# Two transformer blocks on one core: bias loads a unit ahead, u and v in one pass, work spread differently between units

## The chip, the cores and the metric

The kernel runs on one core of one Trainium2 chip. The metric is the device time of one execution in microseconds (us). The core has a matrix engine (TensorE, PE), a vector engine (VectorE, DVE), a scalar engine (ScalarE, ACT), GpSimd (POOL) and SyncE (SP), which here only issues DMAs. Each engine works through its own list of instructions in order; ACT issues some DMAs too.

## The reference, cut to what matters

x is 512 tokens by 1024. The first block adds a mixer, an attention to 256 memory rows and a feed-forward part; the second block has two layers and a second stream, a context of 256 rows, which is computed beside x.

```python
h = rms_norm(x, norm_mix_g)
u, v, q, kv, gl = split(h @ w_in)
a = spatial_gating_unit(gelu(u), gelu(v), ...)
b = nsa_attention(q, kv, gl, ...)
x = x + concat(rms_norm(a), rms_norm(b)) @ w_out
x = x + memory_cross_attention(rms_norm(x), mem, ...)
x = x + square(relu(rms_norm(x) @ w_ff1)) @ w_ff2
for l in range(2):
    m, mc = silu(c) @ w_mod[l] + b_mod[l], silu(c_ctx) @ w_mod[l] + b_mod[l]
    x, xc = ffn(x, m, 0), ffn(xc, mc, 0)
    # mixers on h @ w_in[l]: gated convolution, pooling, and
    # neighbourhood attention: softmax(q k * scale + bias, and context keys)
    x = x + m[5] * mixers(mod_norm(x, m, 1), context keys and values of xc)
    x, xc = ffn(x, m, 2), ffn(xc, mc, 2)      # xc in layer 0 alone
out = rms_norm(x, final_g)
```

mod_norm is an RMS norm with a scale and a shift from the nine rows of m (the conditioning).

## The kernel before, in words

All large products run in three parts: an input h is held as a rounded half and a remainder, each weight tile likewise (whi, wlo), and PE adds whi·h, whi·remainder and wlo·h (L375 to L377 and its kin). A weight tile of 512 KB comes by DMA on SP into one of three buffers (`prefetch`, L330); `ensure` (L334) then lets ACT make whi (L345) and DVE wlo (L346), and `get` (L349) hands out the next tile and sees to the split of the ones behind it. The order of all engines' instructions is the order in which the program calls them; there is no scheduler behind it. So the program works in units (a head and a block of rows, for example), and between two units it puts other work by hand:

- `queue` holds generators; `fill(ns)` (L242) advances the first one until its own estimates of cost sum to ns. A negative cost stops it. The context stream (`ctx_chain`, L1332) is such a generator, and so is the memory's key and value projection (`mem_kv`).
- `after(n, f)` and `sides` are run by `step` (L266), once per unit: postponed pieces and side generators.
- `tick` (L554) does one part of the conditioning: a DMA of 256 KB on ACT's queue into one of two buffers (`wm`) and a product with a sum on DVE (L579). `need_mods` (L595) does as many parts as are lacking where the rows are needed.

In block 1, `project_qk` (L793) makes q and the keys; its `stat` sums squares per head on PE (L848) one step after the product, and `finish_k` (L806) scales the keys and stacks their halves (L817 to L820) in one go. After that v is projected, u is projected as filler between the units of `nsa` (L1003) by `project_u` (L874) with its gelu at the end (L888), and `spatial` (the gating) follows u. Then come the memory attention (`mem_attention`, L1201), and the feed-forward part.

In block 2, `norm_now` (L504) makes a norm of x: sums over columns on PE (L465), a root on POOL and DVE, a spread of the row factors over partitions on PE (L474), then a product on DVE (L496), a sum and cast on ACT (L497) and the remainder on DVE (L499), tile by tile. Between these it fills, and it also calls `ensure`. It is written (l, i) below: norm i of layer l. `attend` (L1670) is the neighbourhood attention of 8 heads by 4 blocks: for each unit `a` computes scores on PE (L1695) and adds the bias on DVE (L1696), `e` is the exponential on ACT (L1703), `bb` transposes on PE (L1710) and copies on ACT (L1712), `cc` multiplies with v (L1724). `pipeline` (L619) lets `bb` and `cc` trail `a` by a given number of units (2 and 2). The bias is loaded in the unit that adds it:

```python
m, pr, bt = self.small(1), tmp(), bias[j % 2]
nc.sync.dma_start(bt[:, :256], self.d["bias"][l, (0, 1, 1, 2)[j], hd])
```

`stack` (L1651) prepares the next head in three steps, one per unit. The first makes halves of q on ACT (L1659) and DVE (L1660) and at once issues two DMAs on SP that copy them crosswise (L1662, L1663). `attend_spread` (L1811) does layer 1's attention with the rest of the mixers as filler.

Of the kernel before, what the change touches and what calls it, by code (L numbers as in the profile page):

```python
# [8 lines left out]
F32 = mybir.dt.float32  # L9
F32R = mybir.dt.float32r  # L10
# [6 lines left out]
T = 512  # L17
TC = 256
# [7 lines left out]
FILL_NSA, FILL_MEM, FILL_MIX, FILL_NA = 1900, 3650, 1350, 900  # L26
FILL_A, FILL_S, FILL_B, FILL_FFN, FILL_END, FILL_U = 1300, 4000, 2500, 0, 700, 4000
# [185 lines left out]

class Body:
    def __init__(self, ctx, tc, d, out, pk, at, order):
        self.ctx, self.tc, self.nc, self.d, self.out, self.pk, self.at = ctx, tc, tc.nc, d, out, pk, at
        enter = ctx.enter_context
        self.const = enter(tc.tile_pool(name="const", bufs=1))
        self.base = enter(tc.tile_pool(name="base", bufs=1))
        self.wp = enter(tc.tile_pool(name="wp", bufs=3))  # L220
        self.tp = enter(tc.tile_pool(name="tp", bufs=5))
        self.sp = enter(tc.tile_pool(name="sp", bufs=10))
        self.pp = enter(tc.tile_pool(name="pp", bufs=5, space=bass.MemoryType.PSUM))
        self.hs = [[self.base.tile([128, 8, n], F32R, tag=f"h{n}{i}", name="h") for i in range(2)] for n in (T, TC)]
        self.order = order
        self.used = []
# [59 lines left out]

    def t2(self, n=512):
        return self.tp.tile([128, 528], F32, tag="t2", name="t2")[:, :n]
# [44 lines left out]

    def ensure(self, i):  # L334
        order = self.order
        while len(self.split) <= min(i, len(order) - 1):
# [4 lines left out]
            hi = self.wp.tile([128, 1024], F32R, tag="whi", name="whi")[:, :nk * nc]  # L341
            lo = self.wp.tile([128, 1024], F32R, tag="wlo", name="wlo")[:, :nk * nc]
# [6 lines left out]
    def get(self, key, tick=1, ahead=2):  # L349
        i = len(self.used)  # L350
        self.used.append(key)
        if self.order is None:
            _, _, nk, nc = self.pk.pieces[key]
            w = [self.wp.tile([128, 1024], F32R, tag=t, name=t)[:, :nk * nc] for t in ("whi", "wlo")]
# [280 lines left out]
    def block1(self):  # L635
# [7 lines left out]
        nc.scalar.copy(warm, warm)  # L643
        for k in range(8):
# [10 lines left out]
        mem = base.tile([128, 8, TC], F32, tag="xc", name="mem")  # L655
# [3 lines left out]
        with tc.tile_pool(name="b1", bufs=1) as self.b1:  # L659
            with tc.tile_pool(name="mix1", bufs=1) as mp:  # L660
# [54 lines left out]
                self.queue += [comp, memkv]  # L715
                for cc in range(2):
                    ps = [self.mm() for _ in range(4)]
                    for half in range(2):
                        self.gemm_tm([(ps[b][:, :256], hh[:, :, b * 128:(b + 1) * 128], hl[:, :, b * 128:(b + 1) * 128])
                                      for b in range(4)], self.get(("v", cc, half)), 4 * half, 8)  # L720
                        self.fill(2000)
                        next(memkv)
                    for b in range(4):
                        nc.scalar.activation(vv[:, b, cc * 256:(cc + 1) * 256], ps[b][:, :256], AF.Gelu_apprx_tanh,
                                             scale=pair[:, 0, b:b + 1])
                self.finish(comp)
                gu = self.project_u(hh, hl, u, vv, rows, pair)
                mh, ml = self.new_h()
                yc = self.keep(2)
                self.chain = self.ctx_chain(yc)  # L730
                sg = self.spatial(u, vv, sgw, mh, ml)
                self.queue.insert(0, gu)
                self.queue.append(self.chain)
                pre = self.ctx_rstd(yc)
                self.sides.append(pre)
                for n, c in enumerate(self.nsa(qs, kh, kl, v2, gates, kc, vc, st_q, mh, ml)):
                    self.fill(FILL_U if n < 10 else FILL_NSA)
                    if self.parts < 48:
                        self.tick()
                    if n == 10:  # L740
                        self.finish(gu)
                        self.sides.append(sg)
                    if n == 14:
                        self.run(pre)
# [48 lines left out]
    def project_qk(self, hh, hl, qs, st_q, kh, kl, gg, x, ss, pair):  # L793
# [12 lines left out]
        def finish_k():  # L806
            for i in range(2):
# [8 lines left out]
                for h in range(2):  # L816
                    nc.scalar.copy(kh[half[h], h, i], k[half[h]])  # L817
                    nc.vector.tensor_copy(kh[half[1 - h], h, i], k[half[h]])
                    minus(kl[half[h], h, i], k[half[h]], kh[half[h], h, i])
                    nc.scalar.copy(kl[half[1 - h], h, i], kl[half[h], h, i].bitcast(F32))  # L820

        for n, m in enumerate((4, 5, 6, 7, 2, 3)):
# [32 lines left out]
            self.after(1, stat)  # L855
# [18 lines left out]
    def project_u(self, hh, hl, u, vv, rows, pair):  # L874
        nc = self.nc
        ln = self.layer_norm(vv, rows)
        for cc in range(2):
            ws = [self.get(("u", cc, half), 1, 2 - half) for half in range(2)]
            for b in range(4):
                next(ln, None)  # L880
                p = self.mm()[:, :256]
                bs = slice(b * 128, (b + 1) * 128)
                for half in range(2):
                    self.gemm_tm([(p, hh[:, :, bs], hl[:, :, bs])], ws[half], 4 * half, 8)
                nc.scalar.activation(u[:, b, cc * 256:(cc + 1) * 256], p, AF.Copy, scale=pair[:, 0, b:b + 1])
                yield 2600
        for b in range(4):
            nc.scalar.activation(u[:, b], u[:, b], AF.Gelu_apprx_tanh)  # L888
# [465 lines left out]
    def ffn2(self, l, f, with_x, with_c, norm_c=None, halves=None):  # L1354
# [103 lines left out]
    def norm_c(self, l, i, slow=True, y=None):  # L1458
# [4 lines left out]
        for _ in self.norm(self.xc, TC, None if y is not None else self.ssc, g, sh, *self.hc, slow=slow, y=y):  # L1463
            yield 1500
# [186 lines left out]
    def stack(self, hd, q_t, k_t):  # L1651
# [9 lines left out]
        halves(q1, q_t[hs, t])  # L1661
        nc.sync.dma_start(q2[os].bitcast(F32), q1[hs].bitcast(F32))  # L1662
# [7 lines left out]
    def attend(self, q_t, k_t, v_t, vc, l, first, mixed, bias, tmp, tmp_t, rows, ready=lambda: True):  # L1670
# [9 lines left out]

        def a(un):
# [10 lines left out]
            nc.sync.dma_start(bt[:, :256], self.d["bias"][l, (0, 1, 1, 2)[j], hd])  # L1692
# [56 lines left out]
        yield from self.pipeline(units, a, bb, cc, 2, 2, e=e)  # L1749
# [173 lines left out]
```

## Time and profile before

| what | value |
|---|---|
| median of 3 runs | 3551.75 us (3551.11 to 3552.49) |
| profiled execution, its time | 3544.91 us |
| its span | 3543.2 us |
| mean granted TensorE clock, as a share of 2.4 GHz | 0.976 |
| PE busy | 3393.7 us, 96% |
| DVE, ACT, POOL busy | 58%, 34%, 3% |

The span goes from the first to the last instruction of one profiled execution; its time is 1.7 us longer than its span. A busy engine is one with an instruction in it, so PE at the lower of its two clocks (1.2 GHz, a granted clock of 0.50) is as busy as at the upper.

### The profile page before, as it was taken

Reading aid. Unit: us, or ns where it says so; the run is one execution under the profiler, and the core shown is the slowest. Engines: PE = TensorE matmul, PEld = TensorE weight load, DVE = VectorE, ACT = ScalarE, POOL = GpSimd, SP = SyncE. Lnnn points to the kernel's source line nnn. Section 1 sums busy time; section 2 is a strip of 40 time slices with the busy share of each in tenths; the row PEclk is TensorE's granted clock in tenths of the full one; section 3 lists DMA queues with packets and bytes.
Section 4 is the critical chain, followed back from the end, with each engine's and each line's share of the span. In section 5 each row is a group of like instructions: output and inputs, shape, how many; then the busy total and the mean of one; then the engine's idle time right before and its main releaser. Section 6 shows DMA issues by size and latency. Waiting matters only on the chain.

```text
span 3543.2 us, 48186 instructions
## 1 busy us (share of the span) xinstructions
PE 3393.7 (96%) x18878; PEld 2960.0 (84%) x18878; DVE 2039.8 (58%) x4231; ACT 1219.0 (34%) x2423; POOL 105.9 (3%) x156
## 2 busy tenths in 40 slices
PE   8979999999999999979999999999999998899999
PEld 6878888888888888878888888888888887778887
DVE  5587666656776677655655555554444454454445
ACT  5445445433332224354421222231222134432222
POOL 1000000000000001000000000100000010000000
PEclk9989999999999999999999999999999999899999
DMA  5533343444444443433333333223323223223332
GB/s 174 185 124 127 112 130 125 141 145 146 146 143 143 144 147 116 155 91 99 102 91 98 98 90 98 75 90 99 96 92 96 68 72 115 61 68 104 101 96 78
DMA packets 143348, 396.79 MB, mean 112 GB/s; under 512 B 16144, under 2 KB 27280, under 8 KB 142608
## 3 DMA queue, kind: packets, MB, share of 16 engines
q1 hardware_dynamic: 94736, 305.61, 27.3%
q10 hardware_dynamic: 48384, 88.10, 8.5%
q8 instruction: 148, 2.42, 0.3%
q14 instruction: 80, 0.66, 0.1%
HBM read 387.36 MB, written 2.10 MB: 110 GB/s over the span
## 4 chain that ended last, share of the span: by engine, by line
PE 84%; DVE 7%; ACT 4%; issue 3%; DMA 2%; POOL 0%; SPq 0%; ACTq 0%; DVEq 0%; POOLq 0%
PE mm L375 19%; PE mm L376 19%; PE mm L377 19%; PE aux L375 5%; PE aux L376 5%; PE aux L377 5%; DVE wlo L346 2%; PE aux L1724 1%; PE mm L404 1%; PE mm L403 1%; PE mm L405 1%; PE mm L388 1%; PE mm L1710 1%; PE mm L389 1%; DMA bias<-in_bias 1%
## 5 line engine op out<-in xcount | busy, mean ns | idle before, releaser
L346 DVE TENSOR_TENSOR wlo<-raw,whi 128x512 fp32r<-128x512 f32 (+1 forms) x1060 | 694.4, 698 | 447.6 <-ACT whi L345 439.3
L345 ACT CAST whi<-raw 128x512 fp32r<-128x512 f32 (+1 forms) x1060 | 599.7, 616 | 938.6 <-issue 773.5
L375 PE MATMUL mm<-h,whi 128*128 128x512 f32 (+1 forms) x2352 | 901.2, 383 | 14.6 <-ACT whi L345 14.6
L376 PE MATMUL mm<-h,whi 128*128 128x512 f32 (+1 forms) x2352 | 895.9, 381 | 0.0
L377 PE MATMUL mm<-h,wlo 128*128 128x512 f32 (+1 forms) x2352 | 894.3, 380 | 0.3 <-DVE wlo L346 0.2
L375 PEld LDWEIGHTS mm<-h,whi 128*128 128x128 f32 x2352 | 449.4, 191 | 97.5 <-ACT whi L345 15.0
L377 PEld LDWEIGHTS mm<-h,wlo 128*128 128x128 f32 x2352 | 448.2, 191 | 84.8 <-DVE wlo L346 1.3
L376 PEld LDWEIGHTS mm<-h,whi 128*128 128x128 f32 x2352 | 449.0, 191 | 79.1 <-issue 0.9
L375 PE MATMUL aux<-h,whi 128*128 128x256 f32 x1056 | 304.0, 288 | 0.0
L376 PE MATMUL aux<-h,whi 128*128 128x256 f32 x1056 | 300.3, 284 | 0.5 <-DVE h L499 0.3
L377 PE MATMUL aux<-h,wlo 128*128 128x256 f32 x1056 | 299.9, 284 | 0.0
L375 PE MATMUL mm<-g,whi 128*128 128x512 f32 (+1 forms) x720 | 277.9, 386 | 0.0
L376 PE MATMUL mm<-g,whi 128*128 128x512 f32 (+1 forms) x720 | 277.7, 386 | 0.0
L377 PE MATMUL mm<-g,wlo 128*128 128x512 f32 (+1 forms) x720 | 276.7, 384 | 0.0
L579 DVE CUSTOM_DVE_ANT_0 wm<-wm,silu_c 128x512 f32<-128x512 f32 x336 | 232.2, 692 | 19.8 <-DMA wm<-in_wmod 13.6
L1384 DVE SCALAR_TENSOR_TENSOR x<-mm,gate,x 128x512 f32<-128x512 f32 x160 | 119.9, 749 | 159.1 <-PE mm L377 159.0
L376 PEld LDWEIGHTS aux<-h,whi 128*128 128x128 f32 x1056 | 203.6, 193 | 5.0 <-DVE h L499 1.3
L375 PEld LDWEIGHTS aux<-h,whi 128*128 128x128 f32 x1056 | 203.7, 193 | 4.1 <-issue 0.3
L377 PEld LDWEIGHTS aux<-h,wlo 128*128 128x128 f32 x1056 | 203.4, 193 | 0.0
L408 ACT CAST g<-t 128x512 fp32r<-128x512 f32 x88 | 54.6, 621 | 396.6 <-DVE t L1430 396.6
L1430 DVE SCALAR_TENSOR_TENSOR t<-t,mm 128x512 f32<-128x512 f32 x88 | 60.6, 688 | 183.7 <-PE mm L377 183.1
L377 PEld LDWEIGHTS mm<-g,wlo 128*128 128x128 f32 x720 | 135.3, 188 | 27.5
(368 smaller groups left out, 4951.1 us busy)
## 6 DMA issues: line engine op xcount, KB each, us to landing
raw<-in_w_a SPq DMA_DIRECT2D x220, 512.0 KB, 3.5
wm<-in_wmod ACTq DMA_DIRECT2D x336, 256.0 KB, 2.7
raw<-in_w_d SPq DMA_DIRECT2D x110, 512.0 KB, 3.5
raw<-in_w_in SPq DMA_DIRECT2D x84, 512.0 KB, 3.6
raw<-in_w_f SPq DMA_DIRECT2D x64, 512.0 KB, 3.5
raw<-in_w_out SPq DMA_DIRECT2D x32, 512.0 KB, 3.5
bias<-in_bias SPq DMA_DIRECT2D x64, 128.0 KB, 2.2
fc<-in_cw SPq DMA_DIRECT2D x8, 512.0 KB, 4.8
```

The costliest lines, as they stand in the source:

```text
L345: self.nc.scalar.copy(hi[:, cs], raw[:, cs])
L346: self.nc.vector.tensor_tensor(lo[:, cs], raw[:, cs], hi[:, cs].bitcast(F32), op=OP.subtract)
L375: mmul(o, wh[:, k, cols], h[:, k], start=s, stop=False)
L376: mmul(o, wh[:, k, cols], l[:, k], start=False, stop=False)
L377: mmul(o, wl[:, k, cols], h[:, k], start=False, stop=e)
L388: mmul(o, wh[:, k], h[:, k], start=n == 0, stop=False)
L389: mmul(o, wl[:, k], h[:, k], start=False, stop=False)
L403: mmul(o, h[:, k0 + k], wh[:, k], start=s, stop=False)
L408: self.nc.scalar.copy(hi, src)
L579: nc.vector.tensor_tensor_reduce(o, w, self.sc[:, s, ks], 1.0, 0.0, OP.mult, OP.add, wm[:, half, s, j % 8:j % 8 + 1])
L1384: nc.vector.scalar_tensor_tensor(xs, o, gate[:, m:m + 1], xs, op0=OP.mult, op1=OP.add)
L1430: nc.vector.scalar_tensor_tensor(hid, hid, 0.5, b, op0=OP.mult, op1=OP.mult)
```

## The change

It has these parts; lines are those of the kernel before, or of the kernel after where it says so.

1. `project_uv` computes v, then u, with the gelu straight out of PSUM, before the attention units, beside the compression, `mem_kv`, the context's sums and the layer norm; `spatial` becomes a side generator from the start of NSA, and the queue holds `mem_kv` and the context chain alone. NSA's fill goes from 1900 (4000 in its first ten units) to 2700 a unit; the context's norm reports 2700 a step in place of 1500.
2. `stat` runs two steps after its product; the stacking of the keys becomes six steps of a side generator.
3. At the start DVE sets the memory tile's first part to 1 and PE multiplies it with itself five times; nobody reads the result, and the memory's load waits for it.
4. `busy(3)`: three products of constants that nobody reads, at up to three places of `norm_now`, if the queue is empty. `ensure` leaves `norm_now` for the feed-forward part's last down products, whose weights (`kept`) are put into two buffers of a pool of their own.
5. In `attend` the bias of unit n+1 is loaded in unit n, and the first one ahead of the loop; the crosswise copies of q are issued one step later, after the halves of k; the lag of `bb` goes from 2 to 3, that of `cc` behind it from 2 to its default 1.

```diff
-FILL_NSA, FILL_MEM, FILL_MIX, FILL_NA = 1900, 3650, 1350, 900
+FILL_NSA, FILL_MEM, FILL_MIX, FILL_NA = 2700, 3650, 1350, 900
...
+    def busy(self, n):
+        p = self.mm()
+        for _ in range(n):
+            self.nc.tensor.matmul(p[:, :256], self.ident, self.cst[:, :256], start=True, stop=True)
...
+    def split_tiles(self, kept, n):
+        pool, bufs = (self.fp, 2) if kept else (self.wp, None)
+        return [pool.tile([128, 1024], F32R, tag="k" * kept + t, name=t, bufs=bufs)[:, :n] for t in ("whi", "wlo")]
...
     def norm_now(self, ready, *args):
+        if not self.queue:
+            self.busy(3)
         self.fill(FILL_A)
         it = self.norm(*args)
         next(it)
+        if not self.queue:
+            self.busy(3)
         self.fill(FILL_S)
         while not ready():
             self.fill(1000)
-        if self.order:
-            self.ensure(len(self.used) + 1)
-        for _ in it:
+        for n, _ in enumerate(it):
+            if n == 0 and not self.queue:
+                self.busy(3)
             self.fill(FILL_B / 4)
...
+        mem = base.tile([128, 8, TC], F32, tag="xc", name="mem")
+        idle = mem.rearrange("p k n -> p (k n)")[:, :512]
+        nc.vector.memset(idle, 1.0)
+        p = self.mm()
+        for _ in range(5):
+            nc.tensor.matmul(p, idle[:, :128], idle, start=True, stop=True)
...
+                pre = self.ctx_rstd(yc)
+                ln = self.layer_norm(vv, rows)
+                for n, _ in enumerate(self.project_uv(hh, hl, u, vv, pair)):
+                    self.step()
+                    next(comp, None)
+                    if n < 4:
+                        next(memkv)
+                    else:
+                        next(pre, None)
+                    if n % 4 == 3:
+                        next(memkv)
+                        next(memkv)
+                    if n > 7:
+                        next(ln, None)
+                for g in (comp, ln, pre):
+                    self.run(g)
                 sg = self.spatial(u, vv, sgw, mh, ml)
-                self.queue.insert(0, gu)
-                self.queue.append(self.chain)
-                pre = self.ctx_rstd(yc)
-                self.sides.append(pre)
-                for n, c in enumerate(self.nsa(qs, kh, kl, v2, gates, kc, vc, st_q, mh, ml)):
-                    self.fill(FILL_U if n < 10 else FILL_NSA)
+                self.sides.append(sg)
+                self.queue += [memkv, self.chain]
+                for c in self.nsa(qs, kh, kl, v2, gates, kc, vc, st_q, mh, ml):
+                    self.fill(FILL_NSA)
...
-                for h in range(2):
-                    nc.scalar.copy(kh[half[h], h, i], k[half[h]])
-                    nc.vector.tensor_copy(kh[half[1 - h], h, i], k[half[h]])
-                    minus(kl[half[h], h, i], k[half[h]], kh[half[h], h, i])
-                    nc.scalar.copy(kl[half[1 - h], h, i], kl[half[h], h, i].bitcast(F32))
+            self.sides.append(stack_k())
...
-            self.after(1, stat)
+            self.after(2, stat)
...
-        ws = [self.get((("d", l, f), len(GROUPS2) - 1, m), 0, 2 - m) for m in range(2)]
+        ws = [self.get((("d", l, f), len(GROUPS2) - 1, m), 0, 2 - m, with_x) for m in range(2)]
         if with_x:
+            if self.order:
+                self.ensure(len(self.used) + 1)
...
-            yield 1500
+            yield 2700
...
         halves(q1, q_t[hs, t])
+        yield
+        halves(kk[:, :T], k_t[hs, t])
         nc.sync.dma_start(q2[os].bitcast(F32), q1[hs].bitcast(F32))
         nc.sync.dma_start(q2[hs].bitcast(F32), q1[os].bitcast(F32))
-        yield
-        halves(kk[:, :T], k_t[hs, t])
         yield
...
+        def load(n):
+            if n < len(units):
+                hd, j = units[n]
+                nc.sync.dma_start(bias[n % 2][:, :256], self.d["bias"][l, (0, 1, 1, 2)[j], hd])
+        load(0)
...
             m, pr, bt = self.small(1), tmp(), bias[j % 2]
-            nc.sync.dma_start(bt[:, :256], self.d["bias"][l, (0, 1, 1, 2)[j], hd])
+            load(4 * hd + j + 1)
...
-        yield from self.pipeline(units, a, bb, cc, 2, 2, e=e)
+        yield from self.pipeline(units, a, bb, cc, 3, e=e)
```

Three places show how the engines' orders move. The first is SP's queue in layer 1's attention, one head of the kernel before: q is the crosswise copy, bias the table that is added, raw a weight tile.

```order
L330 DMA raw<-in_w_out 128x1024
L1662 DMA q_25302<-q_25300 64x512
L1663 DMA q_25302<-q_25300 64x512
L1692 DMA bias<-in_bias 128x256 x4
L330 DMA raw<-in_w_out 128x1024
```

And the same stretch after; bias loads are L1719 there, the copies L1699 and L1700.

```order
L1719 DMA bias<-in_bias 128x256
L1699 DMA q_25314<-q_25312 64x512
L1700 DMA q_25314<-q_25312 64x512
L1719 DMA bias<-in_bias 128x256 x3
L344 DMA raw<-in_w_out 128x1024
```

One bias load of the four has moved ahead of the two copies, and each is now the next unit's.

The second is DVE's order where the context's norm in block 1 begins: L605 scales the norm's gain with the conditioning (sm), L579 is one part of the conditioning. Before:

```order
L579 ISA wm,modp<-wm,silu_c 128x512
L579 ISA modp 128x1
L1104 COPY t_2192<-mm 128x256
L1078 TENSOR_REDUCE sm<-mm 128x2
L1080 TENSOR_SCALAR sm<-sm,st_q 128x2
L970 SCALAR_TENSOR_TENSOR uv<-aux,vecs,uv 128x4x64
L605 SCALAR_TENSOR_TENSOR sm<-mod,vecs 128x8
L1461 COPY kp<-sm 128x8
```

After, where these are L628 and L602, right at the start of the attention units, the last two of seven such parts in a row:

```order
L602 ISA wm,modp<-wm,silu_c 128x512
L602 ISA modp 128x1
L602 ISA wm,modp<-wm,silu_c 128x512
L602 ISA modp 128x1
L609 TENSOR_TENSOR mod<-modp 128x8
L610 TENSOR_TENSOR mod<-mod,vecs 128x8
L628 SCALAR_TENSOR_TENSOR sm<-mod,vecs 128x8
L1496 COPY kp<-sm 128x8
```

The parts lay one by one between units; now the lacking ones stand in a row ahead of the norm's gain.

The third is PE's order at norm (0, 0) of block 2: L465 sums columns, L375 to L377 are context products (fc its input). Before:

```order
L465 MATMUL aux<-cst,ss 128x1
L465 MATMUL aux<-cst,t_9332 128x1
L375 MATMUL aux<-fc,whi 128x256
L376 MATMUL aux<-fc,whi 128x256
L377 MATMUL aux<-fc,wlo 128x256
L375 MATMUL aux<-fc,whi 128x256
```

After, where L484 is the sum, L493 the spread and L407 x's first product of the next part:

```order
L484 MATMUL aux<-cst,ss 128x1
L484 MATMUL aux<-cst,t_10226 128x1
L493 MATMUL aux<-cst,sm 128x128 x4
L407 MATMUL mm<-h,whi 128x512
L408 MATMUL mm<-h,wlo 128x512
L407 MATMUL mm<-h,whi 128x512
```

The context products that stood between the sum and the spread, and behind it, are done elsewhere.

## Rows read from the trace of the kernel before

**Rows 1.** The page's busy times, shares and counts of each engine.

```profile
PE 3393.7 (96%) x18878; PEld 2960.0 (84%) x18878; DVE 2039.8 (58%) x4231; ACT 1219.0 (34%) x2423; POOL 105.9 (3%) x156
```

**Rows 2.** Stages: window, length, busy PE PEld DVE ACT POOL, PEclk, DMA, GB/s.

```profile
16.00:90.00 74.00, 65.20 (x372) 56.66 (x371) 45.05 (x108) 41.87 (x81) 12.41 (x12) 0.93 0.45 147
...
165.00:204.00 39.00, 29.76 (x216) 28.50 (x217) 26.16 (x73) 20.07 (x49) 4.64 (x5) 0.91 0.59 189
204.00:275.00 71.00, 57.11 (x368) 50.83 (x367) 59.90 (x172) 29.79 (x84) 3.13 (x5) 0.86 0.32 97
...
972.00:990.00 18.00, 16.71 (x111) 15.23 (x111) 13.88 (x27) 6.75 (x12) 1.39 (x1) 0.91 0.39 118
...
1489.00:1620.00 131.00, 107.51 (x761) 101.16 (x760) 68.51 (x153) 71.08 (x152) 0.14 (x2) 0.91 0.35 102
...
2286.00:2304.00 18.00, 14.02 (x90) 12.54 (x89) 13.82 (x25) 8.79 (x17) 6.61 (x8) 0.91 0.09 29
...
2957.00:3105.00 148.00, 118.15 (x639) 104.64 (x638) 63.60 (x132) 64.87 (x135) 0.14 (x2) 0.85 0.24 69
3161.00:3175.00 14.00, 9.62 (x43) 8.05 (x43) 8.67 (x15) 4.45 (x7) 1.01 (x1) 0.76 0.05 18
```

**Rows 3.** Waits of PE, whole span: total us, times, longest us.

```profile
PE mm L1710 <- ACT spare L1703: 29.1, 12, 4.8
PE mm L1710 <- ACT p L1703: 19.0, 14, 4.0
...
PE aux L1224 <- ACT t L1220: 2.4, 2, 2.0
```

**Rows 4.** Chain that ended last, 2978 to 2990: start, us, piece.

```profile
2979.58 0.47 SPq L1663
...
2980.14 2.25 DMA bias<-in_bias
```

**Rows 5.** Timeline of layer 1's attention, 2978 to 2985.5: start, us, instruction.

```profile
2982.52 0.69 DVE L1696 CUSTOM_DVE_ANT_0 spare<-mm,bias 128x512 f32<-128x512 f32 x1 [2.97 <-DMA bias<-in_bias]
...
2984.12 0.66 PE L1710 MATMUL mm<-cst,spare 128*128 128x128 f32 x4 [3.71 <-ACT spare L1703]
```

**Rows 6.** Tile bias, DVE's idle time until it landed, layer 1, then layer 0.

```profile
  DMA bias<-in_bias: 21.8, 7
...
  DMA bias<-in_bias: 18.2, 6
```

**Rows 7.** Table by stage around the first stall of layer 1.

```profile
2979.00:2985.00 6.00, 2.29 (x21) 2.09 (x20) 1.64 (x4) 2.04 (x5) 0.00 (x0) 1.00 0.43 109
2985.00:2992.00 7.00, 7.00 (x29) 5.80 (x28) 3.43 (x9) 2.86 (x7) 0.00 (x0) 0.51 0.31 96
```

**Rows 8.** Timeline of the projections, two first matmuls after a wait.

```profile
37.53 1.05 PE L848 MATMUL aux<-cst,t 128*128 128x2 f32 x8 [3.22 <-ACT t L839]
...
83.30 0.60 PE L403 MATMUL mm<-whi,h 128*128 128x280 f32 x1 [5.10 <-ACT whi L345]
```

**Rows 9.** Timeline of the start, PE's second matmul.

```profile
8.28 0.63 PE L376 MATMUL mm<-h,whi 128*128 128x512 f32 x1
```

**Rows 10.** Groups of DVE, 204 to 275: busy us, mean ns | idle before.

```profile
L579 DVE CUSTOM_DVE_ANT_0 wm<-wm,silu_c 128x512 f32<-128x512 f32 x15 | 10.2, 687 | 6.3 <-DMA wm<-in_wmod 6.3
```

**Rows 11.** DMA issues of the page: count, KB each, us to landing.

```profile
wm<-in_wmod ACTq DMA_DIRECT2D x336, 256.0 KB, 2.7
```

**Rows 12.** Timeline of NSA, 217 to 226, PE's longest wait there.

```profile
223.41 1.97 PE L1120 MATMUL aux<-v,t 128*128 128x64 f32 x8 [4.75 <-DVE t L1104]
```

**Rows 13.** Timeline of ACT, 160 to 183, the first of its two table loads.

```profile
163.62 1.28 ACT L888 ACT_TABLE_LOAD   x1
```

**Rows 14.** Groups of PE, 972 to 990, one of three alike.

```profile
L375 PE MATMUL aux<-fc,whi 128*128 128x256 f32 x24 | 7.6, 318 | 0.3 <-DVE xc L1384 0.3
```

**Rows 15.** Timeline of the norm at 2294, DVE and PE.

```profile
2295.08 1.82 DVE L346 TENSOR_TENSOR wlo<-raw,whi 128x512 fp32r<-128x512 f32 x2 [1.05 <-ACT whi L345]
...
2298.37 0.50 PE L388 MATMUL mm<-h,whi 128*128 128x512 f32 x1 [3.97 <-ACT h L497]
```

More of the change, by code (lines that the diff above doesn't have):

```diff
@@ L211, in __init__ @@
         self.sum, self.tail = ap, None
+class Order(list):
+    def __init__(self):
+        super().__init__()
+        self.kept = set()
 class Body:
@@ L225, in __init__ @@
         self.order = order
-        self.used = []
+        self.used = Order()
         self.dmas = 0
@@ L340, in ensure @@
             raw = self.raws.pop(n)
-            hi = self.wp.tile([128, 1024], F32R, tag="whi", name="whi")[:, :nk * nc]
-            lo = self.wp.tile([128, 1024], F32R, tag="wlo", name="wlo")[:, :nk * nc]
+            hi, lo = self.split_tiles(n in order.kept, nk * nc)
             mid = nk // 2 * nc
@@ L347, in ensure, with get @@
             self.split.append((hi.rearrange("p (k n) -> p k n", k=nk), lo.rearrange("p (k n) -> p k n", k=nk)))
-    def get(self, key, tick=1, ahead=2):
+    def get(self, key, tick=1, ahead=2, kept=False):
         i = len(self.used)
         self.used.append(key)
+        if kept:
+            self.used.kept.add(i)
         if self.order is None:
             _, _, nk, nc = self.pk.pieces[key]
-            w = [self.wp.tile([128, 1024], F32R, tag=t, name=t)[:, :nk * nc] for t in ("whi", "wlo")]
+            w = self.split_tiles(kept, nk * nc)
             for t in w:
@@ L714, in block1 @@
                 memkv = self.mem_kv(mem, mss)
[L715 to L727, printed above, removed]
                 mh, ml = self.new_h()
@@ L815, in finish_k, with stack_k @@
                 nc.vector.scalar_tensor_tensor(k, k, gg[:, 1 + i:2 + i], p, op0=OP.mult, op1=OP.mult)
-                for h in range(2):
-                    nc.scalar.copy(kh[half[h], h, i], k[half[h]])
-                    nc.vector.tensor_copy(kh[half[1 - h], h, i], k[half[h]])
-                    minus(kl[half[h], h, i], k[half[h]], kh[half[h], h, i])
-                    nc.scalar.copy(kl[half[1 - h], h, i], kl[half[h], h, i].bitcast(F32))
+            self.sides.append(stack_k())
+        def stack_k():
+            pairs = [(i, h, half[h], half[1 - h]) for i in range(2) for h in range(2)]
+            for n in range(6):
+                if n < 4:
+                    i, h, own, other = pairs[n]
+                    nc.scalar.copy(kh[own, h, i], raw[0][own, i])
+                    nc.vector.tensor_copy(kh[other, h, i], raw[0][own, i])
+                if 0 < n < 5:
+                    i, h, own, other = pairs[n - 1]
+                    minus(kl[own, h, i], raw[0][own, i], kh[own, h, i])
+                if n > 1:
+                    i, h, own, other = pairs[n - 2]
+                    nc.scalar.copy(kl[other, h, i], kl[own, h, i].bitcast(F32))
+                yield
         for n, m in enumerate((4, 5, 6, 7, 2, 3)):
@@ L872, in project_vg, with project_uv @@
         nc.vector.reciprocal(g, g)
[L874 to L888, printed above, removed]
+    def project_uv(self, hh, hl, u, vv, pair):
+        for dst, key in ((vv, "v"), (u, "u")):
+            for cc in range(2):
+                ws = [self.get((key, cc, half), 1, 2 - half) for half in range(2)]
+                for b in range(4):
+                    p = self.mm()[:, :256]
+                    bs = slice(b * 128, (b + 1) * 128)
+                    for half in range(2):
+                        self.gemm_tm([(p, hh[:, :, bs], hl[:, :, bs])], ws[half], 4 * half, 8)
+                    self.nc.scalar.activation(dst[:, b, cc * 256:(cc + 1) * 256], p, AF.Gelu_apprx_tanh,
+                                              scale=pair[:, 0, b:b + 1])
+                    yield
     def compress(self, ksp, w2, kc, vc, rows, gg):
```

9 lines of the change are left out of this document (2 added, 7 removed).

## The prediction

> **What bounds the kernel now.** I read the busy shares first: TensorE (PE) is busy for 3393.7 of 3543.2 us [rows 1]. So at most 149.5 us can come from idle PE; whatever comes beyond that must come from matmuls that ran slow. The table of stages shows both: span less PE busy is idle time, and span times (1 less the granted clock) is what the half clock cost. Two stages stand out [rows 2]: the neighbourhood attention of layer 0 (131 us: 23.5 idle, 11.8 lost to the clock) and of layer 1 (148 us: 29.9 idle, 22.2 lost to the clock). The stages of block 1 from 165 to 275 lose 9.2 + 3.5 and 13.9 + 9.9 us, together 36.5. The waits of PE come next: the attention's transposes (L1710) wait for the exponential (L1703), 29.1 us in 12 waits under one tile name and 19.0 in 14 under another [rows 3].
>
> Then I followed one of these waits back. The chain of waits goes from a copy on SP's queue (L1663, at 2979.58) to the bias load right behind it, which is issued at 2980.14 and lands 2.25 us later [rows 4]; VectorE's (DVE) L1696 starts at 2982.52 after 2.97 us of waiting for it, and PE comes last, at 2984.12, after 3.71 us [rows 5]. The loads are short and their buffers free; they are late because SP issues in order and L1662/L1663 stand ahead of them, waiting for halves of q that ScalarE (ACT) and DVE have only just made. It repeats per head: DVE waits for a bias 7 times, 21.8 us, in layer 1 and 6 times, 18.2 us, in layer 0 [rows 6]. Right after the first such stall the granted clock is 0.51, i.e. the 1.2 GHz level, and PE is busy for all of the 7 us [rows 7]: what it did before was to sit idle for 3.71 us.
>
> **The change, part by part** (plus is time saved).
>
> *Bias a unit ahead, copies a unit later, lag 3.* In the new SP order a head's first bias stands ahead of its two copies, and the copies follow halves made a unit earlier. The load for unit n+1 waits for nothing but the read of unit n-1. What is behind it on SP are the weight loads, which move by a place and have a stage of slack. Layer 1: the whole loss is 29.9 + 22.2 = 52.1; seven bias stalls carry most of it, and some of each unit's chain (DVE, ACT, PE, ACT) stays. I take **+44**; the ends are 22 (21.8, idle alone) and 52. Layer 0 has 35.3 in all, but PE's gaps there are shorter and more, so not each hangs on a bias; by six waits of about 2.3 us, 14, and half of the clock, 6, it is 20, and lag 3 also gives each exponential more time before its transposes: **+23**, ends 14 and 35.
>
> *Projections.* The head statistics are postponed by two steps instead of one; L848 then no longer meets its wait of 3.22 us. The stacking of the keys is spread over six steps; ACT is then free for the weight cast whose lateness cost PE 5.10 us at 83.30 [rows 8]. Idle 8.3, clock loss of the stage 74 x 0.07 = 5.2 [rows 2]; next late are the casts themselves, so not all: **+10**, ends 0 and 13.5. The five products ahead of all else stand in PE's first wait, which ends at about 8 us; the second matmul takes 0.63 us [rows 9]. If the first eight or so give back half of that each, it is 2.5; if the start waits for its loads anyway, nothing; nearest to the latter, as only data released that first wait: **+1**.
>
> *u and v in one pass, and what fills the attention of block 1 (NSA).* The u products used to fill NSA's first ten units. Now the context chain must, and its norm first needs 32 parts of the conditioning: the new DVE order has seven parts in a row at that place. One part is 0.687 us of DVE [rows 10], its 256 KB land in 2.7 us, the median on the page [rows 11], and there are two buffers. So one part per (2.7 + 0.7)/2 = 1.7 us, 12 in all, of which 7 x 0.687 = 4.8 is work taken from later units: 7 net (ends 5 and, with no overlap at all, 24). Then some seven units pass before the first context product, by my count of the new order. An unfilled unit is a chain over DVE: the longest wait on it was 4.75 us [rows 12], the mildest comparable one, a wait on ACT for a square with no filler, is 2.0 [rows 3]. DVE was busy for 59.9 of 71 us there with filler [rows 2], so units are near DVE's pace and I take 2.0; the stage lost 9.9 to the clock on 13.9 idle, a factor of 1.7: 7 x 2.0 x 1.7 = 24. Against this stand the 36.5 now lost. ACT also loads tables twice for the late gelu of u, 1.28 us each [rows 13], on a path to a cast PE waited for: 2.6 back. Sum 36.5 + 2.6 - 24 - 7 = **+8**; the ends are -42 (7 x 4.75 x 1.7 = 57, burst 24) and +34 (units at no cost, burst 5). The Trainium skill, page "ScalarE: Activation LUTs", section "What ACT_TABLE_LOAD costs", adds a drain of about 1380 ns to a load of about 1283. The row agrees on the load, no row here shows the drain; by it the two switches would give 5.3 and the sum 2.7 more.
>
> *Memory attention.* By the new order its context matmuls go from 624 to 168, since NSA at 2700 a unit uses them up. About six units stay without filler, each at 2.0 [rows 3] and a little of clock: **-13**, ends 0 and -48 (6 x 4.75 x 1.7).
>
> *Norms of block 2.* At (0,0) 72 context matmuls (three rows of 24) hid the chain [rows 14]; now none are left, and since a stopped chain remains in the queue the unused products do not appear there either. The price is what an unfilled norm loses now, at 3161: 4.4 idle + 14 x 0.24 = 3.4 of clock, 7.8, less the 1.3 + 1.6 lost already, with some of the chain under the first weights: **-6**. At (0,1) 48 context matmuls go from the same places, but the first weights follow at once: **0**, ends -6 and +1. At (1,0) and (1,1) the splits of the next weights leave the chain, as the last down weights get tiles of their own and no instruction is added: at 2298.37 PE had waited 3.97 us, and the subtractions stood ahead of the norm on DVE until 2296.90, about 2.4 us [rows 15]; with half of the stage's 18 x 0.09 = 1.6 of clock that is some 3.3 each, **+7**, ends 0 and 11. At (1,2) the unused products fill gaps and may hold the clock: three groups of three, each matmul between 0.318 [rows 14] and twice that, so 1 to 2 us in gaps of 1.3 to 1.6: **+3**, ends -2 and 5.
>
> **Sum:** 44 + 23 + 10 + 1 + 7 - 13 - 6 + 1 + 7 + 3 = 77. This is against the profiled execution, 3544.91; the median of the runs is 6.8 us (0.2%) higher, so I set it off there: 3551.75 - 77 = **3475 us**.
>
> **The rivals.**
>
> *A: the gaps go, the clock does not come back.* If low clock follows from the thinness of these stages, not from the stalls, only idle time is won. For: the clock stayed at 0.51 for 7 us with PE busy all through. Against: in the 6 us before, with the stall in them, it was 1.00 [rows 7], so the drop follows the stall. Then the attentions give 24 and 14, the projections 9, NSA 23.1 + 2.6 - 14 - 7 = 5, memory attention -12, the norms -4, 0, 5 and 2: 43 in all, 3509 us. The Trainium skill, page "TensorE: Matmul & The Clock Gate", section "What's actually happening", says that for modelling the ramp penalty is under 1% of a typical kernel span, which would leave no such sum to win; the stages of this trace differ from it (52 us of attention loss hold 34 of clock), so I give it less than it would claim.
>
> *B: starved units, ending slower.* The filler is spent too early. If each of the 7 + 6 unfilled units costs 4.75 us with the factor 1.7, the terms are -42 and -48, the norms -8, and the rest gives 44 + 23 + 11 + 10 = 88: 10 lost, 3562 us. It decides from about 4.3 us a unit. For: DVE is at 84% there [rows 2], and one wait was that long [rows 12]. Against: it was the longest of all.
>
> *C: the bias is no sooner.* If the load ahead still lands late, since its buffer's reader or SP's copies hold it, both attentions give nothing: 77 - 67 = 10, 3542 us. For: two buffers as before. Against: the new order puts nothing but finished work ahead of it.
>
> **Chances.** My forecast 0.68; rival A 0.17; B 0.06; C 0.05; gains beyond 3435 (NSA near its upper end) 0.04. A measurement of this kernel tells apart about 0.2%, 7 us. Faster by more: 0.68 + 0.17 + 0.04 + 0.02 of C = 0.91; within: 0.03 of C; slower: 0.06. The range goes from 3435 (NSA at +34 and memory attention at nothing) to 3520 (rival A with 8 us more lost to unfilled units); it leaves out B, C and the tail.
>
> **What would show it.** In layer 1's attention DVE's waits for the bias fall from 7 to at most 1, the stage from 148 to about 104 us, its clock from 0.85 to 0.97 or more; layer 0 from 131 to about 108. L848 and L403 wait under 1 us. NSA begins with seven conditioning parts 1.9 us apart, PE idle. Memory attention has about six waits of some 2 us on ACT or DVE; norm (0,0) shows 4 us of idle PE; (1,0) and (1,1) wait 1.6 us in place of 4.0. Wrong it would be if the attentions keep their stalls, if their clock stays low without stalls, or if the units of block 1 without filler take over 4 us each.

## The result and the profile after

The changed kernel takes 3603.73 us (3599.74 to 3607.2, 4 runs) against 3552.12 (3551.11 to 3559.39, 4 runs): ratio 1.014, 95% interval 1.0122 to 1.0159. It is slower by 1.4%, far outside the range of the prediction. One execution of a later kernel, its profiled one, took 6834.92 us where the three others took 3660.68 to 3671.68, and is left out of all ratios below.

The busy times on the page of after, beside [rows 1]:

```profile
span 3599.8 us, 48300 instructions
...
PE 3370.0 (94%) x18918; PEld 2936.8 (82%) x18918; DVE 2045.4 (57%) x4232; ACT 1212.3 (34%) x2417; POOL 104.5 (3%) x156
```

PE is busy for less than before, 3370.0 us, in a span 56.6 us longer. So the loss is idle PE, and the clock's line of the page (40 slices, tenths of full speed) shows one place, slices seven and eight, where it is low for longer than anywhere else:

```profile
PEclk9989997599999999999999999999999999999999
```

The waits of PE over the span (total us, times, longest), beside [rows 3]:

```profile
PE mm L1288 <- DVE t L1279: 130.5, 2, 130.2
PE aux L1002 <- DVE uv L1003: 13.1, 2, 12.4
...
PE aux L932 <- DMA fc<-in_cw: 6.9, 2, 4.6
...
PE aux L1765 <- ACT spare L1753: 4.1, 4, 3.3
...
PE mm L1751 <- ACT spare L1744: 0.8, 1, 0.8
```

One single wait has 130.2 of 130.5 us: the transposes of the memory attention (L1288) for a scaling on DVE (L1279). The long waits of the neighbourhood attention's transposes, 29.1 and 19.0 us in [rows 3], have gone: 0.8 us of them remain here (L1751), and the products with v (L1765) wait 4.1 us for the copies. The table of stages of after (columns as in [rows 2]):

```profile
16.00:90.00 74.00, 67.34 (x405) 60.18 (x404) 50.50 (x118) 45.05 (x86) 12.40 (x13) 0.95 0.53 175
184.00:204.00 20.00, 4.80 (x22) 3.04 (x20) 13.27 (x44) 3.78 (x13) 0.00 (x0) 0.61 0.40 110
537.00:590.00 53.00, 48.51 (x320) 43.62 (x320) 31.79 (x89) 22.05 (x51) 3.24 (x4) 0.97 0.36 115
590.00:721.00 131.00, 0.77 (x5) 0.53 (x4) 73.54 (x218) 1.78 (x5) 0.44 (x1) 0.50 0.47 135
721.00:806.00 85.00, 74.33 (x382) 61.37 (x382) 49.63 (x99) 50.62 (x99) 9.68 (x9) 0.90 0.27 84
1148.00:1162.00 14.00, 9.31 (x37) 8.03 (x38) 8.05 (x15) 4.69 (x7) 1.02 (x1) 0.63 0.02 6
1630.00:1743.00 113.00, 109.20 (x870) 105.94 (x868) 74.26 (x165) 77.72 (x168) 0.14 (x2) 0.98 0.42 125
2394.00:2412.00 18.00, 17.62 (x114) 15.60 (x113) 14.40 (x27) 9.18 (x17) 6.14 (x8) 1.00 0.00 1
2956.00:2968.00 12.00, 11.63 (x86) 10.79 (x86) 8.58 (x18) 6.06 (x13) 6.09 (x8) 1.00 0.00 1
3059.00:3178.00 119.00, 112.30 (x741) 101.14 (x740) 68.31 (x144) 71.56 (x151) 0.14 (x2) 0.97 0.32 93
3220.00:3234.00 14.00, 13.56 (x71) 10.89 (x70) 9.50 (x16) 4.98 (x7) 1.02 (x1) 1.00 0.04 17
```

With idle time as length less PE busy, and the clock's cost as length times (1 less the granted clock) as in the prediction, layer 1's attention loses 6.7 + 3.6 = 10.3 us where it lost 52.1, and layer 0's (1630 to 1743) 3.8 + 2.3 = 6.1 where it lost 35.3. The windows of [rows 2] end before the last units of these stages; from the first to the last addition of the bias (L1696, L1737) layer 1 takes 108.1 us where it took 148.7, layer 0 101.4 where it took 130.4. From 590 to 721 PE works for 0.77 of 131 us. DVE is busy for 73.5 of them, and the groups of that stretch say with what:

```profile
L602 DVE CUSTOM_DVE_ANT_0 wm<-wm,silu_c 128x512 f32<-128x512 f32 x68 | 47.1, 692 | 37.9 <-DMA wm<-in_wmod 36.8
L602 DVE CUSTOM_DVE_ANT_0 wj<-wm,silu_c 128x512 bf16<-128x512 f32 x32 | 22.2, 693 | 19.3 <-DMA wm<-in_wmod 19.3
...
L1289 ACT COPY mpt<-mm 128x256 f32<-128x256 f32 x3 | 1.1, 364 | 126.8 <-DMA wm<-in_wmod 126.8
```

L602 is the conditioning: 100 products in a row (68 into wm, 32 into wj, a second product on the same tile), 69.3 us busy and 37.9 + 19.3 us of waiting, nearly all for their 256 KB transfers. The timeline shows how it holds everybody (start, duration, instruction, idle time before it and what ended it):

```profile
588.20 10.70 ACTq L588 DMA_DIRECT2D wm<-in_wmod  x7
...
590.79 0.69 DVE L602 CUSTOM_DVE_ANT_0 wm<-wm,silu_c 128x512 f32<-128x512 f32 x1 [1.76 <-DMA wm<-in_wmod]
...
592.14 0.69 DVE L602 CUSTOM_DVE_ANT_0 wm<-wm,silu_c 128x512 f32<-128x512 f32 x1 [0.65 <-DMA wm<-in_wmod]
...
715.40 0.37 ACT L1289 COPY mpt<-mm 128x256 f32<-128x256 f32 x1 [126.80 <-DMA wm<-in_wmod]
...
720.06 0.35 DVE L1279 TENSOR_SCALAR t<-t,sm 128x256 f32<-128x256 f32 x1
...
720.47 0.69 PE L1288 MATMUL mm<-cst,t 128*128 128x128 f32 x2 [130.24 <-DVE t L1279]
```

DVE waits for a transfer before most products. ACT issues these transfers, and each issue waits for a free buffer, so ACT's next copy starts only at 715.40, after 126.8 us. L1279 stands nine short DVE operations and an exponential on ACT (L1277) behind the last product; it comes at 720.06, and PE goes on at 720.47 after 130.24 us.

Why there? The context chain was ahead of where it used to be: with a fill of 2700 a unit its first feed-forward part was finished in the middle of the memory attention, and its next step is `norm_c(0, 1)`. That norm calls `mods`, and `need_mods` does at once whatever conditioning is lacking: 128 parts are needed there. In the weights of the context's own feed-forward part `get` ticks only up to part 48 (`with_x or self.parts < 48`), and x's own weights had brought the count to 60 by then, so 68 were lacking. In the kernel before the chain reached that norm only at x's norm (0,1), at 1359 us, when x's weights had brought the count to 188.

### The profile page after: what moved, and what is told of

Same layout as the page of the kernel before. It is cut to its first block, busy times and chain, and to the rows that moved or that the text cites. A ratio compares the mean times of both kernels' runs of the same rounds, so it can differ in the third digit from the quotient of the medians.

```text
span 3599.8 us, 48300 instructions
## 1 busy us (share of the span) xinstructions
PE 3370.0 (94%) x18918; PEld 2936.8 (82%) x18918; DVE 2045.4 (57%) x4232; ACT 1212.3 (34%) x2417; POOL 104.5 (3%) x156
## 4 chain that ended last, share of the span: by engine, by line
PE 83%; DVE 7%; DMA 4%; ACT 3%; issue 2%; POOL 1%; SPq 0%; ACTq 0%; DVEq 0%; POOLq 0%
PE mm L394 19%; PE mm L395 19%; PE mm L396 19%; PE aux L394 5%; PE aux L395 5%; PE aux L396 5%; DMA wm<-in_wmod 3%; DVE wlo L363 2%; PE aux L1765 1%; DVE wm L602 1%; PE mm L422 1%; PE mm L424 1%; PE mm L423 1%; PE mm L407 1%; PE aux L1153 1%
## 5 line engine op out<-in xcount | busy, mean ns | idle before, releaser
L602 DVE CUSTOM_DVE_ANT_0 wm<-wm,silu_c 128x512 f32<-128x512 f32 x336 | 231.6, 690 | 64.3 <-DMA wm<-in_wmod 57.9
```

The lines of the kernel that those rows point to most:

```text
L602: nc.vector.tensor_tensor_reduce(o, w, self.sc[:, s, ks], 1.0, 0.0, OP.mult, OP.add, wm[:, half, s, j % 8:j % 8 + 1])
```

## The experiments

Four runs were put beside the kernel before on one chip (3552.2 us, 7 runs). **First, the suspected cost is taken away**: the chain stops ahead of that norm until its conditioning is there, which delays the context's keys and values as well.

```diff
         self.ffn_ready = True
+        while self.mods_done[1] < 5:
+            yield -1
         yield from self.norm_c(0, 1)
```

> The changed kernel, but the context chain stops ahead of norm (0,1) of the context until the conditioning rows it needs are there, so that the 68 parts are not done in a row in the memory attention. My theory: the 130 us gap of PE at 590 is these parts alone and the rest of the change gains about 74 us, so the time falls by 115 to 130, to about 3475 to 3490 (some of it is lost again, as the context's key and value products no longer fill the memory attention). Rival 1: the parts cost about as much wherever they stand, since each takes DVE 0.7 us and a 256 KB transfer, so that most of the gap comes back as smaller waits: 3540 or more. Rival 2: the chain that ran ahead of x is itself what lost the time, by leaving units without filler, and the parts only lay there: then several gaps of 4 us appear in the memory attention and the time is 3500 to 3540.

Measured: 3489.8 us (3486.46 to 3497.58), ratio 0.9826 (0.9807 to 0.9846). That is 114 less than the change and 62 less than the kernel before. The memory attention of this run (window, then waits of PE over the span):

```profile
540.00:663.00 123.00, 101.93 (x496) 80.13 (x497) 65.50 (x159) 59.43 (x123) 12.41 (x11) 0.89 0.22 72
...
PE aux L1002 <- DVE uv L1003: 13.1, 2, 12.3
PE mm L1288 <- DVE t L1279: 11.8, 8, 2.8
```

Rival 1 falls: the parts find room later, between the weights of x, and cost little there. The place of the row decides, not the work. Rival 2 falls too: no gap of 4 us appears in that stage, and the time is below its range. The wait of 130 us has become eight of at most 2.8, 11.8 in all, the price of units without filler. That stage loses 21.1 + 13.5 = 34.6 us, so even without the row it loses some 23 us more than before.

**Second, the same cost is put into the kernel before**, at its ninth unit of the memory attention:

```diff
-            for c in self.pipeline([(h, b) for h in range(4) for b in range(4)], a, bb, cc):
+            for n, c in enumerate(self.pipeline([(h, b) for h in range(4) for b in range(4)], a, bb, cc)):
+                if n == 8:
+                    self.need_mods(0, 4, 1)
                 self.fill(FILL_MEM)
```

> The kernel before with the suspected cost put in: in the memory attention's ninth unit the conditioning is brought to the same row as the changed kernel had it there (100 products on DVE in a row). My theory: PE stands for about 1.3 us per product, 130 us, less little, so 3552 + 115 to 130, about 3667 to 3682. Rival: work that is only moved earlier frees DVE and the queues later, and the net cost is well under the gap: 3600 to 3640.

Measured: ratio 1.0325 (1.0305 to 1.0344), 3552 x 0.0325 = 115 us, at the lower end of the theory; the rival (3600 to 3640) falls. Its trace shows which wait the row makes there:

```profile
PE aux L375 <- ACT whi L345: 116.2, 1, 116.2
```

Here it is a weight cast on ACT, held up by the issues of the row, that PE waits for, and not L1279 behind it on DVE. Both ends agree: 114 without, 115 with the row.

**Third, the attention's part alone on the kernel before, and the change without it** (part 5 of the change, as in its diff).

> The kernel before with the attention's part alone: bias a unit ahead, crosswise copies a step later, lag 3. My theory: layer 1's stage loses about 42 us less and layer 0's about 29, as the two profiles differ, so 3552 - 71 = 3481, with the waits on the bias gone and the clock near 1 in both. Rival: part of the difference in layer 0 came from the other edits (the context products done earlier), so only 3552 - 50 = 3502 or above.

> The changed kernel with the attention's part undone. My theory: the two attentions lose again what they lost before, 3604 + 71 = 3675 (if the parts of the change add up). Rival: with the other edits in place layer 0's waits were smaller anyway: 3604 + 50 = 3654.

Measured: 3482.78 us (ratio 0.9808, 0.9793 to 0.9822) for the part alone, 3671.97 (1.0342, 1.0324 to 1.0359) for the change without it. So it gains 69 on the one kernel and 68 on the other: the parts add up, and both rivals (3502, 3654) fall. Layer 1's attention with the part alone, as a window:

```profile
2938.00:3056.00 118.00, 111.59 (x743) 100.42 (x742) 68.60 (x144) 71.70 (x152) 0.14 (x2) 0.99 0.32 95
```

In the run without it the old waits stand beside the new one:

```profile
PE mm L1288 <- DVE t L1279: 129.1, 2, 128.8
PE mm L1745 <- ACT spare L1738: 29.2, 12, 4.8
PE mm L1745 <- ACT p L1738: 18.8, 14, 3.9
```

The part alone is 7 us below the whole change with its long wait taken away, though the intervals of the two ratios overlap. What the other parts give was tried in four runs beside the kernel before (3550.35, 7 runs): the norms' part (4) on top, then the projections' part (2) too, the change with the norm held back and the projections undone, and a version of it with other fills.

> The kernel before with the attention's part and the norms' part (splits of weights out of the norm, last down weights in tiles of their own, unused products). By the profiles of the run with the attention's part alone and the one that holds the norm back, the stages around norms (1,0), (1,1) and (1,2) lose 17 us less, and the unused products add 9 us of PE work: 3483 - 7 = 3476. Rival: the unused products cost what they give back: 3481 to 3485.

Measured: 3479.89 us (0.9799, 0.9784 to 0.9814), about 3 us less than the attention alone, nearer to the rival; runs differ by 6 us, so this is inconclusive; a later run shows what held it back.

> The changed kernel with the context's norm held back, but the projections' part undone (head sums one step after the product, keys stacked in one go). My theory from the prediction: the two waits of 3.2 and 5.1 us come back, 3490 + 8 = 3498 or more with the clock. Rival: in the changed kernel other waits have taken their place (a load for the compression behind a full queue on SP, 4.2 and 1.9 us), so that the part gains nothing there: 3487 to 3493.

Measured: 3502.9 us (0.9861, 0.9845 to 0.9878) against 3489.8 (0.9826, 0.9807 to 0.9846). The part is worth about 13 us in the changed kernel; the rival falls.

> The kernel before with the parts on the attention, the norms and the projections, without u and v in one pass and without the larger fill (two more steps per product of v bring the stacking to its end in time). Theory: the projections' waits of 3.2 and 5.1 us go: 3476 - 8 = 3468. Rival: a next wait takes their place: 3474 to 3478.

Measured: 3467.4 us (0.9765, 0.9751 to 0.978). That is 12 us below the run without projections: the same part gives 13 and 12 in two kernels. It is also 22 us below the changed kernel with the norm held back (3489.8), from which it differs by having neither part 1 nor part 3: apart from the row, part 1 costs about that much. The waits of PE in this run show what ate the norms' gain (the run before it has the same wait, 8.6 us):

```profile
PE mm L407 <- ACT whi L362: 11.5, 3, 8.6
```

One wait of 8.6 us, at norm (0,1), where the kernel before had 2.6: the splits asked for at the end of the feed-forward part are used up there by the context's products that fill the norm, and nobody asks for the next before x needs them.

> The changed kernel with the context's norm held back, two conditioning parts instead of one with each weight of u and v, and fills of 2300 and 2600 instead of 2700 and 3650, so that every unit of the memory attention has 24 context products. Theory: the 12.4 us gap at the start of the attention units goes with its half clock (12 to 16 us), and the memory attention loses 15 us instead of 33: 3490 - 30 = 3460. Rival: six units without filler at the start of the first attention instead of five, and DVE near its limit there, give it back: 3475 or more.

The edit: in `project_uv` `self.get((key, cc, half), 2, 2 - half)`, fills 2300 and 2600. Measured: 3473.07 us (0.9785, 0.9769 to 0.9802), 17 below the run with the norm held back, not 30: it lies between the theory and the rival. The memory attention does lose less, 12.1 us of idle PE and 6.5 of clock (from 520 to 650). The waits of PE, then ACT's timeline:

```profile
PE aux L948 <- ACT tc L939: 8.8, 1, 8.8
...
PE aux L1002 <- DVE uv L1003: 0.4, 2, 0.2
...
118.04 6.77 ACTq L588 DMA_DIRECT2D wm<-in_wmod  x2
124.86 0.47 ACT L919 ACTIVATE uv<-mm,pair 128x256 f32<-128x256 f32 x1 [11.23 <-DVE modp L602]
```

The gap at the start of the attention units (12.4 us in after, L1002) went to 0.4 in all. But two parts per weight made a new one: two issues of conditioning loads held ACT's queue for 6.77 us, waiting for buffers, and PE waited 8.8 for a copy behind them. In the change and here alike, a row of parts cost PE time where DVE or ACT had something behind it that PE waited for.

**Last, the attention's part taken apart, and the best version**, beside 3550.45 (7 runs). Each piece alone on the kernel before: the load a unit ahead, the copies a step later, the lag of 3.

> The kernel before with the bias loads issued a unit ahead and nothing else of the attention's part (copies where they were, lag 2). My theory: a unit of some 3.6 us is more than the 2.2 us by which the load came late, so nearly all of the attention's gain is here: 3552 - 60 = 3492 or less. Rival (the copies): the load of the next unit still stands behind the two copies that wait for ACT and DVE, so that a head's stall only moves by one unit: 3520 or more. Rival (the lag): the transposes wait for the exponential for reasons of their own: 3510 to 3530.

> The kernel before with the crosswise copies of q one step later alone (bias loaded in its own unit, lag 2). My theory: SP is then not held by the copies, but a bias still lands 2.2 us after its issue in the unit that adds it, with 0.7 us or so of scores to hide it: part of the gain, 3552 - 25 to - 45, 3507 to 3527. Rival: the copies are all that held the loads: 3485 to 3492.

> The kernel before with the transposes three units behind the scores instead of two and nothing else of that part. My theory: the lag hides a late bias in part, as PE has one more unit's work in hand, but SP's stall stays: 3552 - 10 to - 35, 3517 to 3542. Rival: the lag is what makes the difference, 3480 to 3495; or it does nothing: 3549 to 3555.

| piece | median us | ratio (interval) |
|---|---|---|
| load ahead | 3505.32 | 0.9878 (0.9848 to 0.9908) |
| copies later | 3511.03 | 0.9886 (0.9860 to 0.9911) |
| lag 3 | 3523.92 | 0.9924 (0.9901 to 0.9948) |
| all three | 3482.78 | 0.9808 (0.9793 to 0.9822) |

The three gain 45, 39 and 27 us alone and 69 together, so they overlap. The first two remove the same wait, that of DVE for the bias, which was 21.8 and 18.2 us in [rows 6]; over the span, with the load ahead alone and with the copies later alone, it is

```profile
  DMA bias<-in_bias: 1.4, 4
...
  DMA bias<-in_bias: 1.6, 4
```

The copies and the lag came out within their theories; for the load I expected 60 or more, and its rival on the lag (3510 to 3530) comes nearer. With the load ahead alone, layer 1's attention (window, then PE's waits in it) is

```profile
2945.00:3080.00 135.00, 114.54 (x734) 100.20 (x733) 67.56 (x141) 71.47 (x149) 0.14 (x2) 0.97 0.28 82
...
PE mm L1716 <- ACT spare L1709: 17.9, 16, 3.2
```

16 short waits for the exponential remain that the bias had hidden. With the lag alone it is

```profile
2948.00:3097.00 149.00, 125.45 (x742) 110.77 (x742) 68.44 (x144) 71.57 (x152) 0.14 (x2) 0.89 0.25 74
...
PE mm L1710 <- ACT spare L1703: 13.4, 6, 3.2
PE aux L1724 <- ACT spare L1712: 8.4, 6, 6.2
...
  DMA bias<-in_bias: 41.5, 16
```

where the last row is DVE's waiting for the bias over the span, 16 times: the lag hides part of the wait from PE, it does not remove it. The pieces were not tried in pairs. Idle time is alike, 20.5 and 23.5 us, but the granted clock is 0.97 in the first and 0.89 in the second. In these two windows many short waits went with the higher clock, fewer and longer ones with the lower; the windows differ by 14 us.

The best version leaves out u and v in one pass and the larger fills (part 1), keeps the rest, steps twice in each product of v so that the stacking ends in time, and asks for splits in the norm too:

```diff
         while not ready():
             self.fill(1000)
+        if self.order:
+            self.ensure(len(self.used) + 1)
         for n, _ in enumerate(it):
```

> The run with the parts on the attention, the norms and the projections (3467), with the products ahead of all else added, and with the splits also asked for in the norm, where they had been left late at norm (0,1) (a new gap of 8.6 us on a weight cast there). Theory: that gap falls back to the 2.4 us or less of the kernel before, the start gains 1 to 1.5 us, so 3467 - 8 = 3459. Rival: the splits in the norm cost at (1,0) and (1,1) what the part had gained there: 3465 to 3468.

Measured: 3455.24 us (3451.83 to 3459.38), ratio 0.9730 (0.9709 to 0.9751): 95 below the kernel before, 148 below the change; the rival falls. The page of this run, and its waits for that cast:

```profile
PE 3372.4 (98%) x18918; PEld 2941.3 (85%) x18918; DVE 2037.5 (59%) x4232; ACT 1217.2 (35%) x2423; POOL 104.2 (3%) x156
...
PE mm L407 <- ACT whi L362: 2.8, 2, 2.6
```

The wait of 8.6 us is gone, and PE is busy for 98% of the span.

## Why the prediction was wrong, point by point

**The step that failed** is the one on the memory attention: "its context matmuls go from 624 to 168", priced as about six units without filler, each at 2.0, -13, with -48 as the end. Added up over PE's gaps and half of the time at half clock outside them, the stage (475 to 625 before, 537 to 806 after) loses 154 us where it lost about 11: 143 more, 130 of it one wait, ten times the term and three times its end. The wait is for 68 conditioning parts, 100 products in a row on DVE, which the sum does not have. I counted PE's rows in the new order, and asked what a unit without filler costs; I did not ask what else the chain calls when it gets further. The very mechanism was in the text one paragraph earlier: seven parts in a row at the start of the attention units, for the context's first norm. Its second norm needs 128 parts, and DVE's order of the changed kernel has 100 products in a row for it. At the measured pace of the first row, 12.4 us of idle PE for seven parts, 68 parts are 120. None of my rivals was this: rival B had the right side but another mechanism (each unit slow), and the units without filler in the run with the norm held back do wait about as long as I gave them, 11.8 us on L1279. But the term was too small without the row as well: that run's memory attention loses some 23 us more than before, about 10 of them by the clock, which I had put at "a little", and the rest in idle time.

**Attention of layer 1:** +44 forecast, 52.1 - 10.3 = 42 measured. **Layer 0:** +23 forecast, 35.3 - 6.1 = 29 measured; the clock came back there more fully than half. Right in mechanism: DVE no longer waits for the bias in layer 1 at all, only for the scores (idle time of DVE before the addition, by what ended it):

```profile
  PE mm L1736: 4.2, 4
```

Rival A (the clock does not come back) is out: 0.85 to 0.97, 0.91 to 0.98. Rival C is out too. The page "TensorE: Matmul & The Clock Gate" of the Trainium skill (section "What's actually happening") says that for modeling the ramp penalty is under 1% of a typical kernel span. It says so of the slow matmuls at a kernel's start, and the prediction set it against every stretch at half clock: those cost 2.4% of the span before, by its mean granted clock of 0.976. The prediction's "52 us of attention loss hold 34 of clock" also mixes two sums: 34 is the clock's part of both attentions, which lost 87 together.

**Projections:** +10 forecast; the part is worth 12 to 13 (two runs). In the change it shows as less, 14.0 - (6.7 + 3.7) = 3.6 us from 16 to 90, since u and v in one pass brought a wait I had not foreseen, for a load of the compression's weights, which SP issues only right behind a weight tile (L344, at 78.96). SP's issue and PE's wait in after:

```profile
79.34 1.01 SPq L929 DMA_DIRECT2D fc<-in_cw  x2
...
84.80 1.54 PE L932 MATMUL aux<-fc 128*128 128x63 f32 x6 [4.57 <-DMA fc<-in_cw]
```

**u, v and the first attention:** +8 forecast. The row of seven parts is there, 12.4 us of idle PE (I gave 12, 7 net). From 90 us to the memory attention (475 before, 537 after) the loss, added up as for the step that failed, is 47 us before and 45 after, so little of the +8 came. In the run with the norm held back the stages up to the end of the memory attention lose 93 us against 80 before, and the best kernel does without this part.

**The products ahead of all else:** +1 forecast; the clock rises at 7.4 us in place of 12.1, but the first product with whi starts at 8.4 us in place of 7.7, and the 16th at 19.8 in place of 20.1: 0.3. (The 17th gains 1.1, as the head sums that stood ahead of it now come later.)

**Norms:** two rows of before, at (0,1) and (1,1), that [rows 2] does not have:

```profile
1344.00:1368.00 24.00, 19.95 (x107) 17.91 (x106) 19.12 (x38) 11.88 (x22) 4.39 (x6) 0.79 0.21 66
...
2852.00:2868.00 16.00, 12.00 (x75) 10.87 (x75) 12.00 (x22) 8.16 (x16) 6.10 (x8) 0.82 0.11 34
```

(0,0): -6 forecast, 2.9 before, 4.7 + 5.2 = 9.9 after: -7; the -6 does not come out of the figures that the prediction gives for it, 7.8 less 2.9, which make 4.9. (0,1): 0 forecast, 4.1 + 5.0 = 9.1 before, 4.7 + 3.5 = 8.2 after (1518 to 1530): about 0. (1,0) and (1,1): +7 forecast; 4.0 + 1.6 to 0.4, and 4.0 + 2.9 to 0.4: +12. (1,2): +3 forecast, 7.8 to 0.4, but the unused products are PE work themselves: from the norm's gain (L605, L628) to the last norm's first sum the stage takes 362.5 us in place of 364.8, so +2. I had not seen that the splits would be missing at (0,1) when this part stands without the others.

The run is 57 us longer and the memory attention lost 143, so all other stages together gave 143 - 57 = +86, where I had 77 + 13 = 90; that these agree is in part luck, as layer 0 and the norms gave more than I had, and the projections in this kernel, u and v less. With the row of parts at 120 the same sum would have been 77 - 120 = -43, a forecast of 3595 us. The sum line in the text gives the terms for NSA and norm (0,1) as 7 and 1 where their paragraphs say 8 and 0; the total is the same.

## What to carry to other kernels

When work is moved forward in a generator, list all that it calls on the way, on every engine and queue, and look in the new order for long rows of one instruction; a helper that does "whatever is lacking" makes its cost at the caller's place. Price the row by its slowest resource (here, by DVE's waits, the transfers) and then ask what is queued behind it. Keep the part of a change that removes a proven wait separate from parts that only move filler: here the first was worth 69 us alone, and the rest hid it.

## What the runs showed of the hardware that I had not expected

The DMAs issued from ACT's queue held ACT while they waited for their buffers: its next copy came 126.8 us late in the change, and two issues took 6.77 us in a milder case. And idle time of a similar sum went with very different clocks, by how it was cut: with 17.9 us in 16 waits of at most 3.2 the granted clock was 0.97, with 21.8 us in 12 waits of up to 6.2 it was 0.89.

That the pace of the row, 1.3 us a product, is set by the two buffers was not tried. It rests on the 56 us that DVE waits for the transfers in it.
